# A two-layer decoder trunk on one core: the first two products in pair, the start of the loads rearranged, x's last quarter transposed by DMA

## The chip, the core and the metric

The kernel runs on one core of one Trainium2 chip. The metric is the time of one execution on the device, in microseconds (us); the number for a kernel is the median of several executions. Before the change it is 2162.82 us, the median of three runs.

## What is computed

Two layers over a sequence of 256 tokens with 2048 features. Each layer is a token mixer behind an RMS norm and then an MLP with squared ReLU behind an RMS norm, both added to the residual stream. The first layer's mixer, the part that this case is about, is attention with forget gates (FoX):

```python
D_MODEL = 2048; SEQ = 256; HEAD_DIM = 128; FOX_HEADS = 16

def fox_attention(h, w_in, b_f, q_gain, k_gain, w_out):   # h = rms_norm(x, mix_norm_g[0])
    proj = h @ w_in                                       # 2048 x (3*2048 + 16)
    q, k, v, f = jnp.split(proj, [H * dh, 2 * H * dh, 3 * H * dh], axis=-1)
    q = rms_norm(q.reshape(B, S, H, dh), q_gain)
    k = rms_norm(k.reshape(B, S, H, dh), k_gain)
    v = v.reshape(B, S, H, dh)
    log_f = jax.nn.log_sigmoid((f + b_f).astype(jnp.float32))
    c = jnp.cumsum(log_f, axis=1)
    ...
    s = jnp.einsum('bqhd,bkhd->bhqk', q_i, k) * scale
    s = s + jnp.transpose(c_i, (0, 2, 1))[..., None] - c_keys[:, :, None, :]
    p = jax.nn.softmax(jnp.where(causal, s, -jnp.inf), axis=-1)
    return jnp.einsum('bhqk,bkhd->bqhd', p, v)            # then @ w_out
...
def sq_relu_mlp(h, w_up, w_down):
    a = jax.nn.relu(h @ w_up)
    return (a * a) @ w_down
```

The second layer's mixer is a dilated sliding-window attention. All tensors are float32.

## The kernel before, in words

**Products.** Every large product is done in split precision: a weight tile `raw` (two blocks of 128 rows by 512 columns, 512 KB) is cast on ScalarE (ACT) to a rounded `wh` (`hi`, line 308), VectorE (DVE) subtracts it to get `wl` (`lo`, line 309), and TensorE does three matmuls per block of 128 rows and half of the tokens: activation-hi by weight-hi, activation-hi by weight-lo, activation-lo by weight-hi (lines 339 to 341). So one product of 256 tokens x 2048 rows x 512 columns (`product_steps`) is 16 row blocks x 2 halves of the tokens x 3 = 96 matmuls of 128x512. In this text the product matmuls are counted n = 0, 1, 2 and so on from the start. One product holds two of the four `ps_acc` banks of PSUM (`acc`).

**Order of the work.** `Jobs` is a small scheduler that runs while the program is built. Side work (normalization chains, attention heads) is written as Python generators that `yield` either a number of product steps to let pass or the name of a result to wait for. After each row block of a product `tick()` lets due jobs write their instructions. Each engine then does its instructions in that order, and an instruction that must wait holds up all behind it on the same engine. `behind(...)` and `issue_after` fix the order of two instructions.

**Loads.** `plan` lists the weight tiles in order of use; `load` issues one DMA of 512 KB, from SyncE's queue (SP), and `split` casts and subtracts one tile. `RAW_BUFS` and `W_BUFS` buffers bound how far they run ahead. At the start, `hold` keeps the loads after the first ones back: a DVE memset of one element of the target tile, ordered behind the copy of the norm gains (`gained`), stands before each of them.

**The start.** The first 256 KB loads of x and of the first weight tile go out on the queues of SP and ACT. The norm gains (`g_mix`, 16 KB) go out on GpSimd's (POOL) queue, and TensorE turns them into columns (`gain_columns`, line 137). Meanwhile `wake(8)` and later `wake(3)` do 128x128 transposes of an identity into a spare bank. x is in four column quarters `x0` to `x3`. For the first norm each quarter is transposed on TensorE (`ptx`, line 473, 32 transposes of 128x128 in all), and ACT (line 478) and DVE (line 479) multiply by the gain and split it into `hT` hi and lo. The later norms transpose x by DVE's 32x32 stream transposes and a pass of DMAs through DRAM (`transposed_by_dma`).

**The first layer's products.** For each of four groups j of four heads the q product, the k product and the v product follow one another; in group 0 the forget gates (`gate`, 32 matmuls of 128x256, line 639, tile `pf`) lie between q and k. After a product its chain runs beside the next ones: `qk_chain` squares the result on ACT (518), sums it on DVE (522), takes the power on POOL (`rq`, 525), normalizes (DVE 531, `qn`), does stream transposes (DVE 539, `sq`), writes four blocks of 64 KB to DRAM on SP (543), reads them back on POOL's queue (544, into `qn` again), and from there ACT makes `fqT`/`fkT` whole (`w`, 553) and hi (`h`, 560), DVE lo (`l`, 562), for each of two pairs of heads (`fkT_0`, `fkT_1`). The gate's chain makes `pft` (655), log-sigmoids on DVE (659 to 681, `g_z`, `g_u`, `g_s`), a cumulative sum by matmuls (`pc`, 684 to 686), its copy `c_q` (DVE 687), its transpose (`pct`, 691) and `negc` on DVE (693 to 702). `fox_head` starts with three kinds of matmul into `sc_f`: a selection matrix `sel` by `negc` (714), whole q by whole k (620), and the split parts (623). `make_sel(j)` builds `sel`: a POOL memset (747), two POOL selects (749) and a DVE cast (752); it is called at the head of each group's loop, ahead of its q product.

Of the kernel before, what the change touches and what calls it, by code (L numbers as in the profile page):

```python
# [38 lines left out]
CUT = 12  # L39

# [48 lines left out]
def trunk(ctx: ExitStack, tc, x, fox_w_in, fox_b_f, fox_q_gain, fox_k_gain, fox_w_out, dil_w_in,  # L89
# [17 lines left out]
    nc.scalar.activation(warm, warm, AF.Exp)  # L107
# [3 lines left out]
    nc.gpsimd.memset(mhalf, -0.5)  # L111


    spare = ps_sc.tile([P, P], F32, tag="sc", name="spare")

    def wake(times):
        for _ in range(times):
            nc.tensor.transpose(spare, ident, ident)

    wake(8)  # L120
# [20 lines left out]
    mix_rows = gain_rows("g_mix", [mix_norm_g.rearrange(per_chunk, p=P)], nc.gpsimd)  # L141

# [78 lines left out]
    def add_pair(*chunks):  # L221

        for rows in ((0, CUT * P), (CUT * P, D)):
            for w, cols in chunks:
                add(w, rows, cols)
# [6 lines left out]
    for j in range(4):  # L232
        for part in range(3):
            add(fox_w_in[0], (0, D), [(part * D + j * NC, NC)])
# [39 lines left out]
    raws, splits = [], []  # L274

    def load():
# [6 lines left out]
        for c, width in cols:  # L283
            src = w[r:r + RAW_SUB * P, c:c + width].rearrange("(c p) n -> p c n", p=P)
            if i:
                with hold(t[:, 0, 0:1]):
                    issued["load"] = nc.sync.dma_start(t[:, :, at:at + width], src)
            else:

                for part, queue in enumerate((nc.sync, nc.scalar)):  # L290
                    queue.dma_start(t[:, part, at:at + width], src[:, part, :])
            at += width
# [3 lines left out]
    def split():  # L296
# [9 lines left out]
        with behind(*([issued["gained"]] if i == 0 else issued.get("n0", []) if i < 2 * W_BUFS else [])):  # L306
            for part in ([slice(0, 1), slice(1, 2)] if i < 1 else [slice(0, W_SUB)]):
                issued["cast"] = nc.scalar.copy(hi[:, part, :], raw[:, part, :])  # L308
                issued["cut"] = nc.vector.tensor_sub(lo[:, part, :], raw[:, part, :], hi[:, part, :].bitcast(F32))  # L309
        splits.append((hi, lo))  # L310
        state["split"] += 1
# [17 lines left out]
    def product_steps(acc, keys, lhs, steps):  # L329

        for k in steps:
# [4 lines left out]
            for t in range(NT):  # L336
                tok = slice(t * P, (t + 1) * P)
                first, last = k == 0, k == KC - 1
                nc.tensor.matmul(acc[t], ah[:, tok], hi, start=first, stop=False)  # L339
                nc.tensor.matmul(acc[t], ah[:, tok], lo, start=False, stop=False)  # L340
                issued["product"] = nc.tensor.matmul(acc[t], al[:, tok], hi, start=False, stop=last)  # L341
            if i == W_SUB - 1:
                used[0] += 1
                split()
# [8 lines left out]
    def in_pair(new, steps, posts):  # L353
# [75 lines left out]
    def transposed_by_dma(tag, col, n):  # L429
# [3 lines left out]
        for t in range(NT):  # L433
            tile_ = work.tile([P, NC], F32, tag="w", name=f"turned_{tag}_{n}_{t}", bufs=5)
            blocks = dram.tile([4, 32, 4, P], F32, tag="blocks", name=f"blocks_{tag}_{n}_{t}", bufs=4)
            nc.vector.transpose(tile_.rearrange("p (j b r) -> p b j r", j=4, b=4),
                                xt[n][:, t, :].rearrange("p (b j c) -> p b j c", j=4, c=32))
# [3 lines left out]
            nc.sync.dma_start(tile_, blocks.rearrange("j c i x -> (j c) (i x)"))  # L441
            tiles.append(tile_)
        yield 9
# [17 lines left out]
    def norm_chain(tag, col, n, ssp, wait, later):  # L461
        yield wait
        if tag != "n0":
            yield from transposed_by_dma(tag, col, n)
        else:
            for half in range(2):
                pr = n * 2 + half
                pt = ps_tp.tile([P, 2, S], F32, tag="tp", name=f"ptx_{tag}_{pr}")
                with behind(*([issued["product"]] if "product" in issued else [])):
                    for i in range(2):  # L470
                        for t in range(NT):
                            c = (half * 2 + i) * P
                            issued["transposed"] = nc.tensor.transpose(
                                pt[:, i, t * P:(t + 1) * P], xt[n][:, t, c:c + P], ident)
                both = act.tile([P, 2, 2, S], F32R, tag="hT", name=f"hT_{tag}_{pr}", bufs=KC // 2)
                for i in range(2):
                    gc = gain[:, col + pr * 2 + i:col + pr * 2 + i + 1]
                    on_act = nc.scalar.activation(both[:, i, 0, :], pt[:, i, :], AF.Copy, scale=gc)
                    on_dve = nc.vector.scalar_tensor_tensor(both[:, i, 1, :], pt[:, i, :], gc,
                                                            both[:, i, 0, :].bitcast(F32), ALU.mult, ALU.subtract)  # L480
                issued[tag, pr] = issued[tag] = on_act, on_dve
# [428 lines left out]
    first = normed("n0", 0, lambda n: (0, 2, 6, 10)[n], lambda n: (13, 11, 9, 7)[n])  # L910

    def load_x(n):
        for t in range(NT) if n == 0 else [slice(0, NT)]:
            with hold(xt[n][:, 0, 0:1]):
                queue = nc.scalar if t == 1 else nc.sync
                issued["load"] = queue.dma_start(xt[n][:, t, :], xv[:, t, n * NC:(n + 1) * NC])

    def rest():
        while state["split"] - used[0] < W_BUFS:
            split()  # L920
            yield 1

    load_x(0)
    load()
# [7 lines left out]
    del issued["held"]  # L932
# [3 lines left out]
    split()  # L936
    for n in range(1, NX):
        jobs.spawn(first(n))
    jobs.spawn(rest())
    jobs.spawn(more_constants())  # L940
# [3 lines left out]
    for j in range(4):  # L944
        sel = make_sel(j)
# [56 lines left out]
```

## Time and profile before

| what | value |
| --- | --- |
| runs | 2163.41, 2161.27, 2162.82 us; median 2162.82 |
| profiled execution, its own time | 2161.91 us |
| its span on the core | 2160.2 us |
| granted TensorE clock, mean | 1.0 |
| TensorE busy | 2147.8 us, 99% |
| DVE busy | 1397.9 us, 65% |
| ACT busy | 1105.9 us, 51% |
| POOL busy | 74.1 us, 3% |
| data moved | 459.34 MB, mean 213 GB/s |

The profile is one execution. Its times count from the start of its span; the time on the device holds 1.7 us more than the span. A timeline row gives the start, the length, the engine, the line of the kernel, the operation and the tile it writes and reads; `x3` at the end says that three like instructions are drawn together. What stands in square brackets is the engine's idle time before the row and the instruction or DMA that ended it. `PE` is TensorE's matmul side, `PEld` its weight loads, `SPq`, `ACTq` and `POOLq` the sequencers that issue DMAs.

### The profile page before, as it was taken

What the parts mean: (1) busy time and instruction counts of PE and PEld (TensorE: products, weight loads), DVE (VectorE), ACT (ScalarE), POOL (GpSimd) and SP (SyncE); (2) the same over time, 40 slices, a digit from 0 to 9 for tenths busy, and PEclk for the clock granted to TensorE, in tenths of its full rate; (3) what the DMA queues carried; (4) which work ended last, traced back from release to release, by engine and by line L of the source; (5) the groups of instructions that cost most, each with busy time, mean ns of one, the idle gap of its engine ahead of it and who ended that gap; (6) DMA issues with size and microseconds to landing.
All of it is one profiled execution on the core that took longest, in us unless ns stands there. A gap on an engine that the chain in (4) does not pass through costs nothing.

```text
span 2160.2 us, 30057 instructions
## 1 busy us (share of the span) xinstructions
PE 2147.8 (99%) x11208; PEld 1912.6 (89%) x11208; DVE 1397.9 (65%) x1862; ACT 1105.9 (51%) x1545; POOL 74.1 (3%) x92
## 2 busy tenths in 40 slices
PE   9999999999999999999999999999999999999999
PEld 7888888988998998998888888888988988988988
DVE  6777787765655565566668777676655655655664
ACT  6565655644544454455555565546544543544442
POOL 1111000000000000000011010100000000000000
PEclk9999999999999999999999999999999999999999
DMA  7676667766666666667776776758666666666664
GB/s 251 220 225 196 224 201 233 248 203 204 199 203 205 200 201 204 203 199 241 244 242 207 232 226 195 259 177 275 215 204 201 200 204 204 198 203 204 202 210 144
DMA packets 292354, 459.34 MB, mean 213 GB/s; under 512 B 21944, under 2 KB 104432, under 8 KB 292208
## 3 DMA queue, kind: packets, MB, share of 16 engines
q1 hardware_dynamic: 288416, 446.27, 66.1%
q0 software_dynamic: 3232, 10.50, 1.4%
q8 instruction: 87, 1.43, 0.3%
q10 hardware_dynamic: 560, 0.66, 0.1%
q14 instruction: 59, 0.48, 0.1%
HBM read 438.48 MB, written 18.87 MB: 212 GB/s over the span
## 4 chain that ended last, share of the span: by engine, by line
PE 92%; DVE 3%; DMA 2%; issue 1%; ACT 1%; POOL 0%; SPq 0%; DVEq 0%; ACTq 0%; POOLq 0%
PE acc L340 19%; PE acc L341 19%; PE acc L339 19%; PE up_n1a_acc L403 5%; PE up_n3a_acc L403 5%; PE up_n3a_sc L403 3%; PE up_n1a_tp L403 3%; PE up_n1a_sc L403 3%; PE up_n3a_tp L403 3%; PE up_n3a_acc L407 3%; PE up_n1a_acc L407 3%; DMA raw<-in_dil_w_in_dram 2%; DVE wl L309 1%; PE up_n3a_tp L407 1%; PE up_n1a_sc L407 1%; PE up_n1a_tp L407 1%
## 5 line engine op out<-in xcount | busy, mean ns | idle before, releaser
L309 DVE TENSOR_TENSOR wl<-raw,wh 128x1024 fp32r<-128x1024 f32 (+1 forms) x801 | 975.0, 1221 | 686.7 <-ACT wh L308 681.0
L308 ACT CAST wh<-raw 128x1024 fp32r<-128x1024 f32 (+1 forms) x801 | 837.7, 1048 | 931.7 <-PE acc L341 567.4
L339 PE MATMUL acc<-wh,hT_n 128*128 128x512 f32 x896 | 343.0, 384 | 0.5 <-ACT wh L308 0.5
L340 PE MATMUL acc<-wl,hT_n 128*128 128x512 f32 x896 | 339.9, 379 | 0.1
L341 PE MATMUL acc<-wh,hT_n 128*128 128x512 f32 x896 | 339.5, 379 | 0.0
L339 PE MATMUL acc<-wh,aTh_n1a 128*128 128x512 f32 x512 | 194.0, 379 | 0.0
L340 PE MATMUL acc<-wl,aTh_n1a 128*128 128x512 f32 x512 | 194.0, 379 | 0.0
L341 PE MATMUL acc<-wh,aTl_n1a 128*128 128x512 f32 x512 | 194.0, 379 | 0.0
L341 PEld LDWEIGHTS acc<-wh,hT_n 128*128 128x128 f32 x896 | 169.3, 189 | 24.1
L339 PEld LDWEIGHTS acc<-wh,hT_n 128*128 128x128 f32 x896 | 169.6, 189 | 23.4 <-ACT wh L308 0.9
L340 PEld LDWEIGHTS acc<-wl,hT_n 128*128 128x128 f32 x896 | 169.8, 190 | 22.6 <-DVE wl L309 0.4
L339 PE MATMUL acc<-wh,aTh_n3a 128*128 128x512 f32 x480 | 181.9, 379 | 0.0
L340 PE MATMUL acc<-wl,aTh_n3a 128*128 128x512 f32 x480 | 181.9, 379 | 0.0
L341 PE MATMUL acc<-wh,aTl_n3a 128*128 128x512 f32 x480 | 181.9, 379 | 0.0
L403 PE MATMUL up_n1a_acc<-hT_n,wh 128*128 128x512 f32 x512 | 181.6, 382 | 0.0
L403 PE MATMUL up_n3a_acc<-hT_n,wh 128*128 128x512 f32 x512 | 181.6, 382 | 0.0
L407 PE MATMUL up_n1a_acc<-hT_n,wl 128*128 128x256 f32 x512 | 139.6, 273 | 0.0
L407 PE MATMUL up_n3a_acc<-hT_n,wl 128*128 128x256 f32 x512 | 139.6, 273 | 0.0
L341 PEld LDWEIGHTS acc<-wh,aTl_n1a 128*128 128x128 f32 x512 | 96.8, 189 | 13.8
L340 PEld LDWEIGHTS acc<-wl,aTh_n1a 128*128 128x128 f32 x512 | 96.8, 189 | 13.7
L339 PEld LDWEIGHTS acc<-wh,aTh_n1a 128*128 128x128 f32 x512 | 96.8, 189 | 13.6
L403 PEld LDWEIGHTS up_n3a_acc<-hT_n,wh 128*128 128x128 f32 x512 | 96.8, 189 | 13.5
(725 smaller groups left out, 3202.3 us busy)
## 6 DMA issues: line engine op xcount, KB each, us to landing
raw<-in_mlp_w_up_dram SPq DMA_DIRECT2D x256, 512.0 KB, 4.1
raw<-in_mlp_w_down_dram SPq DMA_DIRECT2D x256, 512.0 KB, 4.2
raw<-in_dil_w_in_dram SPq DMA_DIRECT2D x192, 256.0 KB, 4.6
raw<-in_fox_w_in_dram SPq DMA_DIRECT2D x95, 512.0 KB, 4.1
raw<-in_fox_w_out_dram SPq DMA_DIRECT2D x32, 512.0 KB, 4.3
raw<-in_dil_w_in_dram SPq DMA_DIRECT2D x32, 512.0 KB, 4.4
raw<-in_dil_w_out_dram SPq DMA_DIRECT2D x32, 512.0 KB, 4.4
blocks_n<-turned_n SPq DMA_DIRECT2D x96, 64.0 KB, 2.4
```

The source lines that it names most:

```text
L308: issued["cast"] = nc.scalar.copy(hi[:, part, :], raw[:, part, :])
L309: issued["cut"] = nc.vector.tensor_sub(lo[:, part, :], raw[:, part, :], hi[:, part, :].bitcast(F32))
L339: nc.tensor.matmul(acc[t], ah[:, tok], hi, start=first, stop=False)
L340: nc.tensor.matmul(acc[t], ah[:, tok], lo, start=False, stop=False)
L341: issued["product"] = nc.tensor.matmul(acc[t], al[:, tok], hi, start=False, stop=last)
L403: issued["product"] = nc.tensor.matmul(banks[b], hi[:, i, col], in_turn(tokens.rearrange("p x s -> p (x s)"), P // 2), start=first, stop=last)
L407: nc.tensor.matmul(banks[b][:, 0:S], lo[:, i, col], in_turn(tokens[:, 0, :], P // 2), start=False, stop=False)
```

## The change

- The q and k products of group 0 are done in pair: q's row blocks 0 to 11, k's row blocks 0 to 11, then q's 12 to 15 and k's 12 to 15. The gate stands between the two second parts. All four `ps_acc` banks are held until the pair ends. The plan of the loads follows this order. `make_sel(0)` is called behind the pair.
- x's last quarter (row blocks 12 to 15 of the products) is transposed by `transposed_by_dma` in the first norm too, with its last reads on POOL's queue; eight transposes of TensorE go.
- First loads: x's quarter 0 in two halves of columns on SP; the first weight tile's halves on ACT's queue and SP's; the norm gains on ACT's queue. The next loads are paced by memsets of whole target tiles on POOL, each behind the one before, in place of the memsets behind the gains; two more loads follow behind the last of these.
- The first weight tile is cast and subtracted in two halves, the second behind the first pair's `hT`.
- The transposes of a pair of row blocks go to two PSUM banks, one of each pool, in place of one.
- The wake matmuls are 128x512 products of zeros (six, then three), not 128x128 transposes (eight, then three).

```diff
+FIRST_CUT = 12
...
-    spare = ps_sc.tile([P, P], F32, tag="sc", name="spare")
+    spare = ps_sc.tile([P, NC], F32, tag="sc", name="spare")
+    zeros = work.tile([P, NC], F32R, tag="w", name="zeros", bufs=5)
+    nc.vector.memset(zeros.bitcast(F32), 0.0)
...
-            nc.tensor.transpose(spare, ident, ident)
-    wake(8)
+            nc.tensor.matmul(spare, zeros[:, 0:P], zeros, start=True, stop=True)
+    wake(6)
...
-    mix_rows = gain_rows("g_mix", [mix_norm_g.rearrange(per_chunk, p=P)], nc.gpsimd)
...
+        chunks = [(fox_w_in[0], [(part * D + j * NC, NC)]) for part in range(3)]
+        if j == 0:
+            add_pair(*chunks[0:2], cut=FIRST_CUT)
+        for w, cols in chunks[2 if j == 0 else 0:]:
+            add(w, (0, D), cols)
...
-    def hold(first):
+    def hold(whole):
         if "held" not in issued:
             return ExitStack()
-        with behind(issued["gained"]):
-            nc.vector.memset(first, 0.0)
-        return behind(*([issued["load"]] if issued["held"] == [] else []))
+        with behind(*issued["held"]):
+            issued["held"] = [nc.gpsimd.memset(whole, 0.0)]
+        return behind(issued["load"])
...
-    def in_pair(new, steps, posts):
+    def in_pair(new, steps, posts, cut=CUT, between=lambda: None):
         banks = []
         for n in range(2):
             banks.append(new(n))
-            steps(banks[n], range(CUT))
+            steps(banks[n], range(cut))
         for n in range(2):
-            steps(banks[n], range(CUT, KC))
+            steps(banks[n], range(cut, KC))
             jobs.spawn(posts[n](banks[n]))
+            if n == 0:
+                between()
...
-    def transposed_by_dma(tag, col, n):
+    def transposed_by_dma(tag, col, n, queue, steps, *order):
...
-            nc.sync.dma_start(tile_, blocks.rearrange("j c i x -> (j c) (i x)"))
+            queue.dma_start(tile_, blocks.rearrange("j c i x -> (j c) (i x)"))
...
-            yield from transposed_by_dma(tag, col, n)
+            yield from transposed_by_dma(tag, col, n, nc.sync, 9)
+        elif n == NX - 1:
+            yield from transposed_by_dma(tag, col, n, nc.gpsimd, 15, cuts[6], issued["n0"][1])
...
-                pt = ps_tp.tile([P, 2, S], F32, tag="tp", name=f"ptx_{tag}_{pr}")
+                pt = [pool.tile([P, S], F32, tag=x, name=f"ptx_{tag}_{pr}_{x}") for pool, x in ((ps_tp, "tp"), (ps_sc, "sc"))]
...
-    first = normed("n0", 0, lambda n: (0, 2, 6, 10)[n], lambda n: (13, 11, 9, 7)[n])
+    first = normed("n0", 0, lambda n: (0, 2, 5, 7)[n], lambda n: (12, 12, 11, 1)[n])
...
+    nc.sync.dma_start(*halves_x[0])
+    with behind(nc.scalar.dma_start(first_raw[:, 0, :], first_w[:, 0, :])):
+        mix_rows = gain_rows("g_mix", [mix_norm_g.rearrange(per_chunk, p=P)], nc.scalar)
+        nc.scalar.activation(warm, warm, AF.Exp)
+    with behind(nc.sync.dma_start(first_raw[:, 1, :], first_w[:, 1, :])):
+        issued["load"] = nc.sync.dma_start(*halves_x[1])
...
-    issued["held"] = True
-    for what in (load, lambda: load_x(1), load, lambda: load_x(2), load, lambda: load_x(3), load):
+    with behind(issued["load"]):
+        load()
+    issued["held"] = [ready]
+    for what in (lambda: load_x(1), load, load, lambda: load_x(2), load):
         what()
-        issued["held"] = []
     del issued["held"]
+    split_row_block(0)
     jobs.spawn(first(0))
     with behind(issued["transposed"]):
         wake(3)
-    split()
+    with behind(*issued["n0"]):
+        split_row_block(1)
...
+    for what in (load, lambda: load_x(3)):
+        with behind(issued["load"]):
+            what()
...
-        sel = make_sel(j)
+        sel = make_sel(j) if j else None
...
+        if j == 0:
+            in_pair(lambda n: sums(), lambda acc, ks: product_steps(acc, keys_h(tag), lhs_h(tag), ks),
+                    [q_post, k_post], FIRST_CUT, gates)
+            sel = make_sel(j)
+        else:
+            product(keys_h(tag), lhs_h(tag), q_post)
+            product(keys_h(tag), lhs_h(tag), k_post)
```

More of the change, by code (lines that the diff above doesn't have):

```diff
@@ L106, in trunk @@
     nc.gpsimd.memset(warm, 0.0)
-    nc.scalar.activation(warm, warm, AF.Exp)
     ident = const.tile([P, P], F32, name="ident")
@@ L284, in load @@
             src = w[r:r + RAW_SUB * P, c:c + width].rearrange("(c p) n -> p c n", p=P)
[L285 to L291, printed above, removed]
+            with hold(t):
+                issued["load"] = nc.sync.dma_start(t[:, :, at:at + width], src)
             at += width
@@ L305, in split @@
         lo = wpool.tile([P, W_SUB, NC], F32R, tag="wl", name=f"wl{i}", bufs=W_BUFS)
[L306 to L309, printed above, removed]
+        with behind(*(issued.get("n0", []) if i < 2 * W_BUFS else [])):
+            issued["cast"] = nc.scalar.copy(hi, raw)
+            issued["cut"] = nc.vector.tensor_sub(lo, raw, hi.bitcast(F32))
         splits.append((hi, lo))
+        cuts.append(issued["cut"])
         state["split"] += 1
@@ L338, in product_steps @@
                 first, last = k == 0, k == KC - 1
-                nc.tensor.matmul(acc[t], ah[:, tok], hi, start=first, stop=False)
+                with behind(*([issued["product"]] if first and 0 < used[0] < W_BUFS else [])):
+                    nc.tensor.matmul(acc[t], ah[:, tok], hi, start=first, stop=False)
                 nc.tensor.matmul(acc[t], ah[:, tok], lo, start=False, stop=False)
```

72 lines of the change are left out of this document (44 added, 28 removed).

## The prediction

> **What bounds the kernel now.** I read the page first, then TensorE's waits, then the timeline at the two places that the change touches.
>
> ```profile
> span 2160.2 us, 30057 instructions
> ## 1 busy us (share of the span) xinstructions
> PE 2147.8 (99%) x11208; PEld 1912.6 (89%) x11208; DVE 1397.9 (65%) x1862; ACT 1105.9 (51%) x1545; POOL 74.1 (3%) x92
> ```
>
> ```profile
> PE ps_g_mix L137 <- DMA g_mix<-in_mix_norm_g_dram: 2.1, 1, 2.1
> ```
>
> TensorE is busy for 2147.8 of 2160.2 us. So time can only come from TensorE instructions that go away or from the few places where TensorE waits, and time is lost where a new wait is made. In the list of its waits the longest that the change touches is the one above, for the norm gains at the start; a second, for the first FoX head, is shown with its rows further down. The whole stake is a few microseconds in 2162, and 0.2% is 4.3 us, about what a measurement of this kernel can tell from no change: faster is under 2158.5, slower over 2167.15.
>
> The start, from the timeline (start, length, engine, line, tile; idle time before it and what ended that), engine by engine: TensorE, GpSimd, ACT, DVE.
>
> ```profile
> 6.62 0.31 PE L137 MATMUL ps_g_mix<-ident,g_mix 32*128 32x32 f32 x1 [2.11 <-DMA g_mix<-in_mix_norm_g_dram]
> 6.86 1.11 PE L473 MATMUL ptx_n<-ident,x 128*128 128x128 f32 x4
> 7.76 0.85 PE L118 MATMUL spare<-ident 128*128 128x128 f32 x3
> 8.53 0.80 PE L339 MATMUL acc<-wh,hT_n 128*128 128x512 f32 x1
> 9.12 0.63 PE L340 MATMUL acc<-wl,hT_n 128*128 128x512 f32 x1
> 9.55 0.59 PE L339 MATMUL acc<-wh,hT_n 128*128 128x512 f32 x1
> 9.97 0.38 PE L340 MATMUL acc<-wl,hT_n 128*128 128x512 f32 x1
> 10.19 0.59 PE L341 MATMUL acc<-wh,hT_n 128*128 128x512 f32 x2
> ...
> 19.91 0.46 PE L339 MATMUL acc<-wh,hT_n 128*128 128x512 f32 x1
> ```
>
> ```profile
> 1.42 0.66 POOL L130 DMA_DIRECT2D g_mix<-in_mix_norm_g_dram  x1 [0.33 <-issue]
> ...
> 3.03 1.34 POOL L749 TENSOR_SCALAR_AFFINE_SELECT self<-self 128x512 f32<-128x512 f32 x2
> ```
>
> ```profile
> 8.01 0.47 ACT L478 ACTIVATE hT_n<-ptx_n,gain 128x256 fp32r<-128x256 f32 x1 [0.68 <-PE ptx_n L473]
> ...
> 11.91 1.04 ACT L308 CAST wh<-raw 128x1024 fp32r<-128x1024 f32 x1 [0.17 <-DMA raw<-in_fox_w_in_dram]
> ```
>
> ```profile
> 4.41 0.44 DVE L752 CAST sel<-self 128x512 fp32r<-128x512 f32 x1 [4.41 <-POOL self L749]
> ...
> 45.03 1.22 DVE L309 TENSOR_TENSOR wl<-raw,wh 128x1024 fp32r<-128x1024 f32 x1
> ```
>
> The gain row's DMA, issued on POOL at 1.42, releases TensorE at 6.62. The first product is at 8.53. Starts 9.55 and 9.97 lie 0.42 us apart, 9.97 and 10.19 only 0.22 (to more digits 0.2157, the pitch I use): the clock came up at 9.97, after TensorE had been at work steadily since 6.62. The row at 19.91 is product matmul n = 36, counting the 128x512 product matmuls from 0.
>
> **Part 1, the start.** The gain rows now go out on ACT's hardware queue, behind a 256 KB half of the first weights. I bound their landing by these rows:
>
> ```profile
> x<-in_x_dram ACTq DMA_DIRECT2D x1, 256.0 KB, 4.0
> ...
> g_mix<-in_mix_norm_g_dram POOLq DMA_DIRECT2D x1, 16.0 KB, 5.2
> ```
>
> From above: no sooner than before, 6.6. From below: an ACT-queue DMA issued at 0.81 has landed after 4.0, at 4.8. The ACT-queue row is the nearest, so I take 5.0. Then come the gain transpose (0.24, from 6.62 to 6.86), the first x transposes (0.90, to 7.76) and three 128x512 wake matmuls at the cold 0.42 (1.28, they were 128x128): first product at 7.4, 1.1 earlier. The Trainium skill, "DMA: Bandwidth & Descriptors", section "Latency and other measured facts", gives 600 ns to the first byte for a hardware queue and about 1 us for GpSimd's. By that figure the gain rows would come only 0.4 us earlier, at 6.2, the first product would be at 8.6, and 1.2 us of this part's gain would be gone; the 4.0 against the 5.2, with the issue 0.6 earlier, says more than that, and I keep the rows.
>
> From 7.4 to n = 36: 36 products x 0.2157 = 7.8; 20 transposes in that stretch (16 before) at 0.109, half of a 256-column pitch, = 2.2; cold pitch up to the same 9.97, half of 2.6 = 1.3 (0 if the six wide wake matmuls bring the clock up before, which the narrow eight did not); and a wait for the second weight chunk. That one is now split behind the first pair's hT: 0.47 + 0.47 + 1.04 + 1.22 = 3.2 us of ACT and DVE against some 2.2 us of TensorE work, so 1.0 (0 to 2). Sum 19.7, against 19.91: -0.2. And of x's 32 transposes eight are gone and four that came later are done by then: 12 x 0.109 = 1.3 less afterwards. **Early gain 1.5 us**, between -1.1 (gain rows no sooner than 6.6, the second chunk's wait at 2) and 4.0 (gain rows at 4.8, the clock up, no such wait).
>
> What the quarter's new path needs costs nothing as long as it lies beside TensorE's matmuls: two stream transposes, eight block DMAs on SP, two DMAs on POOL, 8 ACT and 8 DVE operations of 128x128 for x's last quarter. That quarter holds rows 12 to 15, which the pair uses only after row 11 of k, and by the order of the queues I estimate 3.6 us in hand; if that cover is gone, the third rival has its price. Likewise the third and fourth ps_acc banks: v's first product now waits until q's result is read out, with some 0.6 us to spare by my estimate; if it waits, that time is part of the DVE time counted next and not added to it.
>
> **Part 2, head 0.** The first head's scores need the k product normalized, and that chain runs mainly on DVE:
>
> ```profile
> 65.15 0.36 DVE L529 TENSOR_SCALAR rq_('fk', 0)_723<-rq_('fk', 0)_723,rstd_n 128x4 f32<-128x4 f32 x2 [1.78 <-POOL rq_('fk', 0)_723 L525]
> ...
> 72.75 0.38 DVE L562 TENSOR_TENSOR fqT_1l<-sq_('fq', 0)_0_525,fqT_1h 128x256 fp32r<-128x256 f32 x1
> ```
>
> ```profile
> 73.19 0.53 POOL L747 MEMSET self<- 128x512 f32 x1 [8.08 <-DVE fqT_1l L562]
> 73.80 2.54 POOL L749 TENSOR_SCALAR_AFFINE_SELECT self<-self 128x512 f32<-128x512 f32 x2
> 76.29 0.60 POOL L544 DMA_DIRECT2D qn_('fk', 0)_0_771<-blocks_('fk', 0)_0_777  x1
> ```
>
> ```profile
> 81.91 0.51 ACT L553 ACTIVATE fkT_0w<-qn_('fk', 0)_0_771,gain 128x256 f32<-128x256 f32 x1 [1.87 <-DMA qn_('fk', 0)_0_771<-blocks_('fk', 0)_0_777]
> ```
>
> ```profile
> 85.26 0.33 PE L714 MATMUL sc_f<-negc,sel 128*128 128x384 f32 x1
> 85.43 0.38 PE L620 MATMUL sc_f<-fkT_0w,fqT_0w 128*128 128x128 f32 x2
> 86.96 0.38 PE L623 MATMUL sc_f<-fkT_0h,fqT_0h 128*128 128x256 f32 x1 [1.15 <-ACT fkT_0h L560]
> ```
>
> From the split at 45.03 to the end of fqT_1l at 73.13 DVE has 28.1 us of queued work: q's chain, k's chain, the gate's small operations and nine weight splits. Then POOL builds the next selection table (memset and two selects), and only behind it issues k's block read; the read takes 5.6 and ACT begins fkT_0w at 81.91. So fqT_1l to fkT_0w is 8.8 us. TensorE reaches the head at 85.26 and waits there 1.15 us in the row at 86.96, with smaller gaps before and behind it 1.7 us in all.
>
> Before, TensorE had 96 k products and the gate between q's end and k's end. In the pair q ends at n = 167 and k at n = 191, only 24 products later, and the two chains fall on DVE together. Let E be q's end. DVE's list until fqT_1l is the same 28.1, and: +1.3, because the wait for POOL's rq of k (1.78 in the row) and that of q are no longer both covered by splits that are there to be done; +0.41 and +0.44, the copy of the gate's result and the cast of the first selection table (4.41 row), which now lies behind the pair; -0.6, part of q's square sums that come before E. It starts 1.25 after E, when ACT has squared q's first half and the split in hand is done. So fqT_1l ends at E + 30.9, fkT_0w starts 8.8 later at E + 39.7, and TensorE can do its head product at E + 40.1 (half a microsecond of ACT). TensorE without a wait gets there after 147 products x 0.2157 = 31.7, nine gate matmuls at half that, 1.0, and the gate's and head's small matmuls, 1.8: E + 34.5. **It waits 5.6 us** (3.0 to 7.0), of which about 1.0 falls at the gate's transpose pct, whose operand c_q is copied on DVE behind rq of k and a split, and 4.6 in one stretch at the head. The old 1.7 goes: **+3.9**. What is late next is the weighted sum of head 0 and head 1's transposes, since two heads' DVE work is then bunched: +0.2, between 0 and 0.8.
>
> The waiting instruction stands in TensorE's one queue, so everything behind it, the v products too, waits; DVE and ACT do splits meanwhile, and come out of the wait with more chunks in stock, so nothing else is lost. Paced loads move SP's later loads earlier than the gain did; they were not the bound after n = 36 and I cost them at nothing.
>
> **Sum.** The profiled run took 2161.91 (span 2160.2 and 1.7 around it). -1.5 + 3.9 + 0.2 = +2.6, so 2164.5. The median of before, 2162.82, is 0.9 above that run: forecast 2165.4, inside 0.2%.
>
> **The rivals.**
>
> *The idle stretch costs the clock too (slower).* After the start TensorE's longest stretch without work in this trace is the 1.15 us at 86.96, and no row shows what a longer one does. At the start the clock was down until TensorE had worked 3.35 us (6.62 to 9.97); a second such stretch at half clock costs 1.7, and up to double if the gate comes late, so +2.5: 2167.9, over the bound. It decides from the idle length at which the gate closes, against my 4.6. The Trainium skill, "TensorE: Matmul & The Clock Gate", section "What's actually happening", says that the clock halves after about 3.4 us of idle, counted in a free-running window. By that rule a 4.6 us stretch closes the gate only in those phases in which a whole window fits into it, and a wait of under 3.4 never does; the trace's 1.15 us without a change agrees and cannot decide. Chance 0.24.
>
> *The k chain is in time (faster).* If the selects take 1.34 as at 3.03 instead of 2.54, the block read takes about 3.8 instead of 5.6, as this row of the second group of heads has it, and two of the nine splits fall behind the chain (1.2 each), 5.4 us go and the head does not wait.
>
> ```profile
> qn_('fq', 1)_0_1276<-blocks_('fq', 1)_0_1282 POOLq DMA_DIRECT2D x1, 256.0 KB, 3.8
> ```
>
> ```profile
> GB/s 0 52 297 328 175 0 41 233 239 367 377 411 383 400 392 392 392 382 382 283 61 17 85 252 367 398 400 398 385 252 210 328 293 18 234 197 221 192 234 177
> ```
>
> Then -1.5 - 1.7: 2159.6; with the clock up early at the start (1.3 more) 2158.3. Against it: all three must happen, and in this trace the rows beside the chain show none of them. Chance 0.22, half of it under the bound.
>
> *Loads come late.* The GB/s row (1.25 us a slice, first 50 us) shows the DMA engines at about 400 for most of 11 to 24 us. x's last quarter now goes out to blocks and back in, 1.05 MB more, 2.6 us at that rate, in just this stretch, and the weight load for rows 10 and 11 stands on SP's queue behind the loads of the gate's weights and bias. By the order of the queues I estimate 1 to 2 us in hand; if that is too much by as much, TensorE waits 1 to 3 us before n = 144: about 2167.4. Chance 0.10.
>
> The change might also do nothing of what it says: the first products may start no earlier if the gain rows land at 6.2 or later. That takes 1.2 off the gain, 2166.6, and lies inside the forecast's own range.
>
> **How the numbers follow.** Forecast 0.44, its own range 2163 to 2168 (the early gain down to its half or up to 2.5 and the wait between 4 and 7, not all at the worst end at once), with 0.10 of it over 2167.15. Clock rival 0.24, of it 0.19 over. Loads 0.10, 0.07 over. In time 0.22, 0.12 under 2158.5. Slower 0.10 + 0.19 + 0.07 = 0.36, faster 0.12, the rest 0.52. The range leaves out 0.12 below 2158.5 and some 0.08 above 2169.5, the clock rival with both its bounds.
>
> **What would show it.** Right: the gain's transpose on TensorE near 5.0 and the first product near 7.4; eight fewer ptx transposes; a wait of 4 to 5 us before the first head's fkT_0w product, released by ACT, and one of about 1 before pct; n = 36 near 19.7. Wrong: no wait at the head; product starts 0.42 apart behind the wait; a wait of a product for wh released by a raw DMA between 20 and 45 us; or a gain transpose no earlier than 6.2.

## The result, and the profile after

The changed kernel takes 2167.88 us (median of 8 runs, 2165.64 to 2169.53), the kernel before 2161.82 (8 runs, 2160.04 to 2163.67). The ratio is 1.0028, 95% interval 1.0017 to 1.0039: 6.1 us slower, or 0.28%. The forecast was 2165.4 with a range of 2158.5 to 2169.5; the time is that of its clock rival, and over the 0.2% that the prediction called slower (chance 0.36). The profiled run took 2167.86, its span is 2166.0.

The page of the changed kernel, and below it the list of TensorE's waits (in total, how often, longest):

```profile
span 2166.0 us, 30067 instructions
...
PE 2151.1 (99%) x11198; PEld 1914.9 (88%) x11198; DVE 1400.6 (65%) x1862; ACT 1105.4 (51%) x1549; POOL 79.8 (4%) x98
```

```profile
PE sc_f L631 <- ACT fkT_0w L564: 4.6, 1, 4.6
PE ps_g_mix L139 <- DMA g_mix<-in_mix_norm_g_dram: 2.1, 1, 2.1
...
PE pct L702 <- DVE c_q L698: 1.0, 1, 1.0
```

Two entries of 1 us or more are new in kind: 4.6 at the first head's product of whole q and k, and 1.0 at the gate's transpose (the 1.5 left out is the first wake matmul's, 2.5 before). TensorE's busy time went up by 3.3 us with ten matmuls fewer. By the windows view 1.5 of that lies before product n = 192, where the wake matmuls are wider, and 2.7 between n = 300 and 360. The timeline around the first head, in that stretch, shows slow matmuls:

```profile
88.45 0.38 PE L340 MATMUL acc<-wl,hT_n 128*128 128x512 f32 x1
93.46 0.79 PE L631 MATMUL sc_f<-fkT_0w,fqT_0w 128*128 128x128 f32 x2 [4.63 <-ACT fkT_0w L564]
93.90 0.77 PE L341 MATMUL acc<-wh,hT_n 128*128 128x512 f32 x1
94.47 0.63 PE L339 MATMUL acc<-wh,hT_n 128*128 128x512 f32 x1
94.90 0.63 PE L340 MATMUL acc<-wl,hT_n 128*128 128x512 f32 x1
...
97.88 0.50 PE L341 MATMUL acc<-wh,hT_n 128*128 128x512 f32 x1
98.22 0.38 PE L339 MATMUL acc<-wh,hT_n 128*128 128x512 f32 x1
```

From 94.47 to 97.88 products start 0.43 apart, twice 0.2157. The windows view puts the granted clock beside it (the column after POOL's busy time; then the DMA engines' busy share and GB/s):

```profile
88.00:90.00 2.00, 0.83 (x4) 0.38 (x2) 1.11 (x1) 0.00 (x0) 0.90 (x2) 1.00 1.02 391
90.00:92.00 2.00, 0.00 (x0) 0.00 (x0) 0.00 (x0) 0.00 (x0) 0.00 (x0) 0.83 1.02 333
92.00:94.00 2.00, 0.54 (x3) 0.55 (x3) 0.00 (x0) 1.10 (x3) 0.00 (x0) 0.50 1.01 396
94.00:96.00 2.00, 2.00 (x7) 1.64 (x6) 1.34 (x3) 1.39 (x3) 0.00 (x0) 0.50 0.23 86
96.00:98.00 2.00, 2.00 (x6) 1.55 (x6) 0.65 (x1) 0.00 (x0) 0.00 (x0) 0.50 0.13 11
98.00:100.00 2.00, 2.00 (x12) 1.81 (x11) 0.50 (x1) 1.58 (x3) 0.00 (x0) 0.97 0.72 251
```

0.83 in the second row means that the clock fell to half at about 91.3; by the 0.97 in the last it came back at about 98.1. What releases the head is the chain that the prediction followed, on POOL (table, then the block reads) and ACT:

```profile
84.73 0.53 POOL L758 MEMSET self<- 128x512 f32 x1 [6.63 <-DVE fqT_1l L573]
85.33 2.48 POOL L760 TENSOR_SCALAR_AFFINE_SELECT self<-self 128x512 f32<-128x512 f32 x2
87.77 0.59 POOL L555 DMA_DIRECT2D qn_('fk', 0)_0_770<-blocks_('fk', 0)_0_776  x1
```

```profile
92.90 0.51 ACT L564 ACTIVATE fkT_0w<-qn_('fk', 0)_0_770,gain 128x256 f32<-128x256 f32 x1 [6.17 <-DMA qn_('fk', 0)_0_770<-blocks_('fk', 0)_0_776]
```

At the start, TensorE and the DMA issues on ACT:

```profile
6.59 0.28 PE L139 MATMUL ps_g_mix<-ident,g_mix 32*128 32x32 f32 x1 [2.14 <-DMA g_mix<-in_mix_norm_g_dram]
...
8.99 0.63 PE L339 MATMUL acc<-wh,hT_n 128*128 128x512 f32 x1
...
12.26 0.72 PE L339 MATMUL acc<-wh,hT_n 128*128 128x512 f32 x1
12.82 0.38 PE L340 MATMUL acc<-wl,hT_n 128*128 128x512 f32 x1
13.03 0.38 PE L341 MATMUL acc<-wh,hT_n 128*128 128x512 f32 x1
```

```profile
0.81 0.45 ACTq L938 DMA_DIRECT2D raw<-in_fox_w_in_dram  x1
1.29 0.48 ACTq L132 DMA_DIRECT2D g_mix<-in_mix_norm_g_dram  x1
```

The gains release TensorE at 6.59, where it was 6.62 before, and the fast pitch begins only at 12.82.

Where the 5.8 us between the two spans lie, by the start of the same product matmul n (lines 339 to 341) in both traces (after less before): at n = 192, when both have done the same products, +0.3; at n = 300, behind pct, +1.5; at n = 360, from where the order of TensorE's instructions is the same, +7.6; at the end +5.9. The last 1.7 come back in the second layer's attention (n = 3860 to 4670), where the profile of before has a second wait at sc_d (0.6) and a short one at ptp_d (0.1) which the profile after does not have. The change has no part in that: no profile of an experiment has the 0.6 either, not even that of `before_gain` (below), which has the instructions of before there and stands at -0.06 against it at n = 2600 and at -1.6 at n = 4670. Whether the kernel before often waits so, or only in this execution, is open. From 300 to 360 the gaps over the usual pitch come to some 5.9 of these 6.1: 4.8 of wait (the row's 4.63 and the restart), 0.3 behind it, 2.2 of slow pitch in ten products, 0.4 at the split scores, less the 1.8 of before.

### The profile page after: what moved, and what is told of

Read it like the earlier page. It is cut to its first block, busy times and chain, and to the rows that moved or that the text cites. A ratio compares the mean times of both kernels' runs of the same rounds, so it can differ in the third digit from the quotient of the medians.

```text
span 2166.0 us, 30067 instructions
## 1 busy us (share of the span) xinstructions
PE 2151.1 (99%) x11198; PEld 1914.9 (88%) x11198; DVE 1400.6 (65%) x1862; ACT 1105.4 (51%) x1549; POOL 79.8 (4%) x98
## 4 chain that ended last, share of the span: by engine, by line
PE 96%; DVE 2%; DMA 1%; issue 1%; ACT 0%; POOL 0%; SPq 0%; ACTq 0%; POOLq 0%; DVEq 0%
PE acc L340 20%; PE acc L341 20%; PE acc L339 20%; PE up_n1a_acc L406 5%; PE up_n3a_acc L406 5%; PE up_n1a_sc L406 3%; PE up_n1a_tp L406 3%; PE up_n3a_sc L406 3%; PE up_n3a_tp L406 3%; PE up_n3a_acc L410 3%; PE up_n1a_acc L410 3%; PE up_n3a_tp L410 1%; PE up_n3a_sc L410 1%; PE up_n1a_tp L410 1%; PE up_n1a_sc L410 1%; DVE wl L307 1%
## 5 line engine op out<-in xcount | busy, mean ns | idle before, releaser
L307 DVE TENSOR_TENSOR wl<-raw,wh 128x1024 fp32r<-128x1024 f32 x799 | 973.9, 1223 | 684.0 <-ACT wh L306 681.1
L306 ACT CAST wh<-raw 128x1024 fp32r<-128x1024 f32 x799 | 835.6, 1048 | 933.0 <-PE acc L341 569.2
```

The costliest lines, as they stand in the source:

```text
L306: issued["cast"] = nc.scalar.copy(hi, raw)
L307: issued["cut"] = nc.vector.tensor_sub(lo, raw, hi.bitcast(F32))
```

## The experiments

Each is a kernel of its own, compared with the kernel before on the same chip; the changed kernel itself is at 2167.88. The kernel before had medians of 2161.4 to 2161.7 in these comparisons. Differences between two changed kernels are by their medians, a rough measure: the interval of each against before is 2 to 3 us to either side.

**Selection tables behind k's reads** (`sel_late`). The POOL memset of the next table is ordered behind the last block read:

```diff
-            nc.gpsimd.dma_start(qn[t], blocks...)
+            issued["read"] = nc.gpsimd.dma_start(qn[t], blocks...)
...
-        nc.gpsimd.memset(sf, 0.0)
+        with behind(*([issued["read"]] if j else [])):
+            nc.gpsimd.memset(sf, 0.0)
```

> The changed kernel, with POOL's build of the next selection table (memset and two selects) forced behind the two block reads of k. TensorE's order is that of the changed kernel. Theory A (the head's wait is set by the chain DVE fqT_1l, POOL's table, POOL's block read, ACT; and its 4.63 us of idleness closes the clock): the read is issued about 3.1 us earlier, the wait before the first head's fkT_0w product falls from 4.63 to about 1.5, no product behind it starts 0.43 apart, and the time falls by 3.1 + 2.3 = 5.4, from 2167.9 to about 2162.5. Theory B (the read is limited by the DMA engines, not by its issue): the read lands where it did, nothing gained, 2167 to 2168. Theory C (the clock loss has nothing to do with the length of the idle stretch): 3.1 gained, slow pitch stays, 2164.8.

2162.88 us, ratio to before 1.0006 (0.9997 to 1.0015): 5.0 won, and no longer to be told from before. POOL, and TensorE's timeline at the head:

```profile
84.13 0.59 POOL L555 DMA_DIRECT2D qn_('fk', 0)_0_770<-blocks_('fk', 0)_0_776  x1 [7.41 <-DMA blocks_('fk', 0)_0_776<-sq_('fk', 0)_0_723]
```

```profile
89.28 0.49 PE L631 MATMUL sc_f<-fkT_0w,fqT_0w 128*128 128x128 f32 x2 [1.83 <-ACT fkT_0w L564]
89.52 0.46 PE L341 MATMUL acc<-wh,hT_n 128*128 128x512 f32 x1
89.82 0.38 PE L339 MATMUL acc<-wh,hT_n 128*128 128x512 f32 x1
```

The read now waits for its blocks and not for POOL, the head waits 1.83, and the products behind it keep the pitch of 0.2157. Theory A holds: the table cost about 3 us in the chain, and the rest of the 5.0 is the clock. That the clock stayed up behind the head is seen in this one execution. Five of the 11 runs have a mean granted clock of 0.999, which is what one stretch of 3.4 us at half clock makes of 2160 us; in the profiled one, one of the five, that stretch lies at the start, from 7.8 to 11.2.

**Work in the wait** (`fill`). The first head's first matmul is done 20 times more.

```diff
-        yield (3 if j == 3 else 4) * hh + 2
+        yield (3 if j == 3 else 4) * hh + (2 if h else 3)
...
+            for _ in range(0 if h else 20): nc.tensor.matmul(ps[:, 0:3 * P], sel[:, hh, :], in_turn(negc, P // 2), start=True, stop=True)
```

> The changed kernel, with the first head's first matmul (128x384) done 20 times more, each overwriting the last, one row block later, so that TensorE works for 3.3 of the some 5 us in which it would wait; the end of the wait stays where ACT's fkT_0w sets it. Theory A (idleness closes the clock): an idle stretch of about 2 us is left, products behind it start 0.216 apart, and the time falls by 1.3 to 2.3 (the split scores now stand nearer behind the wait and may wait up to 1.0), to about 2166. Rival (the clock falls for another reason, such as the kind of work or the DMA load): slow pitch stays, no change, 2168 or more.

2170.38 us, 1.0038 (1.0026 to 1.0051): by the medians 2.5 worse than the changed kernel, not better (the two intervals overlap). The edit moved the head's split scores up behind the whole product, where they wait for ACT too:

```profile
92.86 0.49 PE L631 MATMUL sc_f<-fkT_0w,fqT_0w 128*128 128x128 f32 x2 [1.88 <-ACT fkT_0w L564]
93.10 0.46 PE L339 MATMUL acc<-wh,hT_n 128*128 128x512 f32 x1
93.40 0.38 PE L340 MATMUL acc<-wl,hT_n 128*128 128x512 f32 x1
93.61 0.38 PE L341 MATMUL acc<-wh,hT_n 128*128 128x512 f32 x1
96.15 0.58 PE L634 MATMUL sc_f<-fkT_0h,fqT_0h 128*128 128x256 f32 x1 [2.16 <-ACT fkT_0h L571]
96.52 0.63 PE L339 MATMUL acc<-wh,hT_n 128*128 128x512 f32 x1
```

As a test of "one long stretch" it failed, but its timeline says more than the time does: behind the first wait of 1.88 the pitch is fast (93.40, 93.61), behind the second of 2.16 it is slow (96.52 on), though neither is half as long as 4.63. So one unbroken wait is not needed. Nor is a loaded DMA, which the rival named: the clock falls in this row of the windows (0.94), and the DMA engines are idle in it (busy share 0.01).

```profile
94.00:96.00 2.00, 0.00 (x0) 0.00 (x0) 1.48 (x3) 2.00 (x5) 0.00 (x0) 0.94 0.01 3
```

That it goes by how little is done in a stretch of some 3.4 us fits these rows; it is a reading of them, with its figures in the next section, and not a test.

**Heads later** (`heads_later`). The first group's heads begin four row blocks later:

```diff
-        yield (3 if j == 3 else 4) * hh + 2
+        yield (3 if j == 3 else 4) * hh + (6 if j == 0 else 2)
```

> The changed kernel, with the four heads of the first group begun four row blocks (24 products, 5.2 us) later. Theory A: the wait of 4.63 at the first head goes or is under 1, the clock stays up, and 4.6 + 2.3 are won: about 2161, if the heads' ends find room in the next q product. Rival (the bunched DVE work of four heads and of the next group makes new waits behind): waits at the transposes or products of the later heads of 2 to 4 us, 2163 to 2165.

2169.79 us, 1.0035 (1.0021 to 1.0048). Nothing was won; the time is over the rival's 2163 to 2165 too. Its waits:

```profile
PE sc_f L634 <- ACT fkT_0h L571: 3.1, 1, 3.1
...
PE ptp_f L605 <- DVE s_f L744: 1.6, 1, 1.6
...
PE sc_f L631 <- ACT fkT_0w L564: 1.4, 1, 1.4
```

The scheduler that orders TensorE's queue now put the split scores close behind the whole product, so the wait of 4.6 became 1.4 and 3.1, with three products between. The clock fell all the same (half from 96.3 to 103.2 in its windows), and a wait at a later head's transposes, the 1.6, came on top. That is more than the rival foresaw, which had waits at the later heads alone.

**Gains first** (`gain_first`). The gains' DMA goes ahead of the first weight half on ACT's queue:

```diff
-    with behind(nc.scalar.dma_start(first_raw[:, 0, :], first_w[:, 0, :])):
-        mix_rows = gain_rows("g_mix", [...], nc.scalar)
-        nc.scalar.activation(warm, warm, AF.Exp)
+    mix_rows = gain_rows("g_mix", [...], nc.scalar)
+    with behind(issued["rows"]): first_half = nc.scalar.dma_start(first_raw[:, 0, :], first_w[:, 0, :])
+    with behind(first_half): nc.scalar.activation(warm, warm, AF.Exp)
```

> The changed kernel, with the norm gains' DMA ahead of the first weight half on ACT's queue, not behind it. In the changed kernel the gains release TensorE at 6.59, no earlier than before. Theory A (the 16 KB stood in the queue behind 256 KB): the gain transpose starts between 3.5 and 5.0, the first product 1.5 to 2.5 earlier than at 8.99 unless the first weight half, 0.5 later, holds it, and the time falls by 1 to 2, to about 2166.4. Theory B (16 DMA engines busy with 1 KB pieces delay every queue alike): the gain transpose still starts after 6.0 and the time stays at 2167.5 to 2168.5.

2166.44 us, 1.0023 (1.0014 to 1.0033), 1.4 under the changed kernel by the medians; this was not resolved between the two directly. The DMA view (KB each, median us to landing) and ACT's timeline:

```profile
g_mix<-in_mix_norm_g_dram ACTq DMA_DIRECT2D x1, 16.0 KB, 2.6
```

```profile
6.55 0.62 ACT L958 CAST wh<-raw 128x512 fp32r<-128x512 f32 x1 [3.26 <-DMA raw<-in_fox_w_in_dram]
```

The gains land 2.6 after their issue at 0.81, so at 3.4, and the gain transpose is at 4.38, right behind the wake matmuls. So it is the place behind the 256 KB, with an issue 0.48 later, that held them in the changed kernel. Whether the queue's order did it or the load that all DMA engines have by then is not separated: in the kernel before the gains were alone in POOL's queue, issued at 1.42, and released TensorE at 6.62 too. The first product then waits 1.5 for what the weight half holds up, and starts at 7.59.

**The start alone** (`start_only`): no pair (q, gate, k as before, plan and tables too), x's last quarter on TensorE and the order of the first norm as before, everything else of the change kept.

```diff
-        if j == 0:
-            add_pair(*chunks[0:2], cut=FIRST_CUT)
-        for w, cols in chunks[2 if j == 0 else 0:]:
+        for w, cols in chunks:
...
-        elif n == NX - 1:
-            yield from transposed_by_dma(tag, col, n, nc.gpsimd, 15, cuts[6], issued["n0"][1])
...
-            in_pair(lambda n: sums(), ..., [q_post, k_post], FIRST_CUT, gates)
-            sel = make_sel(j)
+            product(keys_h(tag), lhs_h(tag), q_post)
+            gates()
+            product(keys_h(tag), lhs_h(tag), k_post)
```

> The changed kernel without the pair and with x's last quarter transposed by TensorE again: of the change only the new first loads, the gains on ACT's queue, the wide wake matmuls and the two banks for transposes are left. Theory A (the start is worth little either way, as the gains land no earlier and the first product comes at 7.7 to 9.0 by the clock's phase; the loss is the pair's): 2161 to 2163 against 2161.7 of before, the first head's wait as before, under 2. Rival (the start itself loses, by the 1 KB pieces of x's two column halves and the later clock): 2163 to 2165.

2160.67 us, 0.9997 (0.9988 to 1.0006): no difference that this measurement resolves, and by the median just under both ranges. The first head waits 1.0. The start did not lose the 6 us.

**The pair alone** (`pair_alone`): the kernel before with q and k in pair, plan, gate and first table as in the change.

```diff
+            in_pair(lambda n: sums(), lambda acc, ks: product_steps(acc, keys_h(tag), lhs_h(tag), ks),
+                    [q_post, k_post], gates)
+            sel = make_sel(j)
```

> The kernel before, with the first q and k products in pair behind row 12 and the first selection table behind the pair; start and transposes as before. Theory A (the pair brings q's and k's chains onto DVE together): the wait of some 4.6 at the first head's fkT_0w product and one of 1 at pct appear, the clock falls behind it in most runs: 2161.7 + 6 to 8, 2168 to 2170. Rival (the loss needs the new start or the DMA path of x's last quarter, whose SP and POOL transfers delay k's blocks): wait under 3, 2162 to 2165.

2166.88 us, 1.0025 (1.0016 to 1.0035). Its waits and one row of its windows:

```profile
PE sc_f L625 <- ACT fkT_0w L558: 4.9, 1, 4.9
```

```profile
92.00:96.00 4.00, 3.32 (x9) 2.77 (x10) 1.99 (x3) 2.49 (x5) 0.00 (x0) 0.50 0.31 119
```

The pair alone makes the wait and the clock loss, and 5.4 of the 6 us; that is about 1 under theory A's 2168 to 2170. The wait at pct is not in its list: that part of theory A was wrong.

**The quarter on TensorE** (`pe_quarter`): the changed kernel without the two lines that send x's last quarter through `transposed_by_dma`.

> The changed kernel with x's last quarter transposed by TensorE, the pair and all else kept. Theory A (the DMA path puts some 1.4 us of stream transposes and eight short subtractions onto DVE, ahead of the norm's square sums, and so makes the 1.2 us wait at pct): the wait at pct goes, TensorE has 8 transposes of 0.109 more, the first head's wait of 4.6 stays with the clock loss behind it: 2167.9 - 1.2 + 0.9 less the chain's head start of 0 to 1, 2166.5 to 2167.6. Rival (the pct wait is the pair's own, since c_q stands behind k's chain): pct wait stays at 1.0 to 1.2, 2168.5 to 2169.

2166.74 us, 1.0023 (1.0014 to 1.0032). The list of TensorE's waits has 4.5 at sc_f and no pct. So the DMA path, which takes eight transposes off TensorE (0.9), is what makes pct wait (1.0). By the medians it costs 1.1, which the intervals do not resolve. The likely way, argued and not tested alone, is DVE's queue: two stream transposes and, in this row of the changed kernel's groups from 40 to 60 us, eight subtractions:

```profile
L459 DVE SCALAR_TENSOR_TENSOR hT_n<-turned_n,gain,hT_n 128x128 fp32r<-128x128 f32 x8 | 2.2, 347 | 0.0
```

What pct waits for, `c_q`, stands on DVE behind k's `rq` and a split in the changed kernel (the first two rows); in `pe_quarter` (the last row) DVE waits for TensorE there.

```profile
74.55 0.36 DVE L540 TENSOR_SCALAR rq_('fk', 0)_731<-rq_('fk', 0)_731,rstd_n 128x4 f32<-128x4 f32 x2 [1.78 <-POOL rq_('fk', 0)_731 L536]
...
75.95 0.18 DVE L698 COPY c_q<-pc 128x32 f32<-128x32 f32 x1
```

```profile
73.75 0.19 DVE L696 COPY c_q<-pc 128x32 f32<-128x32 f32 x1 [0.73 <-PE pc L695]
```

**The changed kernel mended** (`pair_best`): `sel_late`, `gain_first` and pct two row blocks later (`yield 3` for `yield 1` behind `c_q`).

> The changed kernel with the two edits that gained, the selection tables behind k's block reads and the gains first on ACT's queue, and the gate's transpose pct two row blocks later. Theory A (the three are independent): 2167.9 - 5.0 - 1.4 - 1.2 = 2160.3; no wait at pct, the first head's wait under 1.5, the clock stays up. Rival (each only moves the same wait: head 0 then waits for DVE, whose list is as long as before): 2161.5 to 2163.

2161.94 us, 1.0005 (0.9996 to 1.0013). The rival held: the wait moved. With pct later, `negc` is later on DVE, and the head's first matmul waits for that:

```profile
88.11 0.57 PE L725 MATMUL sc_f<-negc,sel 128*128 128x384 f32 x1 [2.69 <-DVE negc L713]
88.48 0.63 PE L340 MATMUL acc<-wl,hT_n 128*128 128x512 f32 x1
```

```profile
88.00:90.00 2.00, 1.89 (x5) 1.64 (x6) 1.67 (x1) 0.42 (x1) 0.59 (x1) 0.55 1.00 394
```

And 2.69 us were enough for the slow clock in this execution: the granted clock is 0.55 in the two us behind the wait.

**The kernel before with the same two edits** (`before_two`), and each alone (`before_gain`, `before_sel`). The gains go first on ACT's queue, ahead of its halves of x and of the first weights; ACT's table load moves behind these; the tables as in `sel_late`.

```diff
-    mix_rows = gain_rows("g_mix", [mix_norm_g.rearrange(per_chunk, p=P)], nc.gpsimd)
+    mix_rows = gain_rows("g_mix", [mix_norm_g.rearrange(per_chunk, p=P)], nc.scalar)
...
     load()
+    with behind(issued["first"]): nc.scalar.activation(warm, warm, AF.Exp)
```

> The kernel before with two edits of the same kind: the gains first on ACT's queue (ACT's table load behind its three loads), the selection tables behind k's block reads. Theory A: the gain transpose starts at 4.4 to 5.0 and the first product 1.0 to 1.5 earlier; the first head's 1.7 goes; 2161.7 - 1.2 - 1.7 = 2158.8, under before and under the changed kernel. Rival (x's first half, now second on ACT's queue, holds the transposes, and the first head then waits for DVE): 2160.5 to 2161.7.

> The kernel before with the gains first on ACT's queue alone (the table load behind ACT's three loads). Theory A (the two edits of before_two are independent): gain transpose at about 4.3, first product about 7.5, 2161.5 - 1.3 = 2160.2. Rival (the earlier start is eaten by weight loads that come no earlier): 2161.0 to 2161.7.

> The kernel before with the selection tables behind k's block reads alone. Theory A: the first head's waits of 1.7 go, nothing new: 2161.5 - 1.7 = 2159.8. Rival (the reads land no earlier, or later groups lose what the first wins): 2161.0 to 2162.

`before_two` 2158.36 us, 0.9987 (0.9978 to 0.9996); `before_sel` 2159.25, 0.9990 (0.9981 to 0.9999); `before_gain` 2160.36, 0.9992 (0.9983 to 1.0001), not resolved. By the medians -2.2 and -1.1 alone and -3.1 together: they add up within the noise. What the gains first are worth alone is open: in `before_gain`'s profile the first product starts 0.6 earlier, but n = 36 at the same time as before: TensorE waits 1.8 for x's half, and the fast pitch begins at 11.5, not at 10.0. In `before_two` n = 36 is 1.2 earlier, no wait at the first head is left in the list, and the start reads (TensorE):

```profile
4.29 0.31 PE L136 MATMUL ps_g_mix<-ident,g_mix 32*128 32x32 f32 x1 [0.39 <-DMA g_mix<-in_mix_norm_g_dram]
4.54 0.48 PE L472 MATMUL ptx_n<-ident,x 128*128 128x128 f32 x1
5.87 0.90 PE L472 MATMUL ptx_n<-ident,x 128*128 128x128 f32 x3 [0.85 <-DMA x<-in_x_dram]
```

Here x's half, now second on ACT's queue, takes back 0.85 of what the gains won.

**The change's start with both edits** (`start_two`): `start_only` with `sel_late` and `gain_first`.

> The start of the change without pair and without the DMA path, with both gaining edits: gains first on ACT's queue, selection tables behind k's block reads. Theory A (all add up): 2160.7 - 1.4 - 1.7 = 2157.6, as good as or better than before_two's 2158.4. Rival (the first weight half, second on ACT's queue, holds the first product, as it did in gain_first by 1.5): 2158.5 to 2159.5.

2158.63 us, 0.9984 (0.9975 to 0.9993): the rival's range, no better than `before_two`, with a wait of 1.4 before the first product. Both are under the kernel before and under the changed one.

## Why the prediction was right or wrong

- **The head's wait** was right in mechanism and size: 1.0 at pct and 4.6 at the head were forecast, 1.0 and 4.63 measured. The steps of the chain hold too: q's last product ends at 53.6 (the prediction's E), fqT_1l 31.0 later (forecast 30.9), and the head's product starts 39.9 later (forecast 40.1). `pair_alone` shows that the pair makes the second wait, and `sel_late` that POOL's table lies in its chain. One reason was wrong: at pct, c_q does stand behind k's rq and a split on DVE, as forecast (74.55, 75.95), but that comes with x's quarter on DVE. Without it k's rq is done by 69 and pct does not wait (`pe_quarter`). So the 1.0 that came out right there is luck.
- **The clock** was the rival at 0.24, and it came. Its condition, 4.6 us of idleness being too much, held; its price of 2.5 was close to the 2.2 measured. What failed is the step from a wait to its price in the forecast: the idle stretch alone was charged. All 8 runs of the changed kernel have a mean granted clock of 0.997 to 0.999 where 17 of 20 runs of before have 1.000 (one stretch of 3.4 us at half clock makes 0.999, the two of the changed kernel's profile 0.998). So the likeliest case should have had it. The Trainium skill, "TensorE: Matmul & The Clock Gate", section "What's actually happening", speaks of an idle window of about 3.4 us; by that rule waits of under 3.4 cost no clock. Here 2.69 did in one execution and two waits of 1.88 and 2.16 with five matmuls between them in another, while 1.83 alone, in `sel_late`, did not, so the measurement speaks for a window in which little was done. An estimate from the windows view, over the 3.4 us before each fall at the head: 0 to 1.1 us of work in seven profiles, with 1.6 in the stretch of `sel_late` that kept its clock (steps of 3.41 from its fall at 7.8). The limit is not fixed by that: at the start the clock fell in four profiles behind stretches with 1.3 to 1.9 us of work (`sel_late`, `pe_quarter`, `pair_best`, `start_two`).
- **The early gain** failed: -1.5 forecast; +0.3 at n = 192 in the profile after. Two terms were mis-sized. The gains were put at 5.0 by the row of an ACT-queue DMA that was first in its queue, and came at 6.59: that they stand behind 256 KB was said but not priced (`gain_first`: landed at 3.4, transpose at 4.38). And the clock was to come at 9.97 as before; it came at 12.8 here. The four profiles with this same start code (`after`, `sel_late`, `fill`, `heads_later`) have n = 192 at +0.3, -1.2, -0.4 and -0.4 against before, with the lasting fast pitch beginning between 10.5 and 12.8. So the start, with its fewer transposes, gains some 0.4 on average, and single profiles differ by 1.5. The rule of the Trainium skill on first bytes ("DMA: Bandwidth & Descriptors", "Latency and other measured facts"), by which the gains come at 6.2 by the prediction's estimate, was nearer than my row here; but with the gains first in the same hardware queue they landed at 3.4, which 0.4 us would not give.
- **The transposes**: ten matmuls fewer in all (eight transposes, two wake matmuls), as read from the diff. That their cover costs nothing was wrong: with the DMA path came the wait at pct (`pe_quarter`), about as long as what was saved; that it comes by the 16 short operations and two stream transposes is argued.
- **What comes behind the head** (+0.2) was 0.4, and **late loads** did not happen: no product waits for a weight load between 20 and 45 us.

The range held, but the size did not: +2.6 was forecast, and 6.1 came. Two of the prediction's own signs of being wrong were seen: products 0.43 apart behind the wait, and a gain transpose later than 6.2. From profile to profile the miss is some 3.3 us: 2.2 of clock left out, 1.8 from the early gain (-1.5 forecast, +0.3 measured) and 1.0 in smaller terms, less the 1.7 that came back in the second layer. The forecast's time is off by 2.5 only, because it started from a median of three runs, 0.9 above the profiled run, that 8 runs put 1.0 lower. That the measured time equals the clock rival's to 0.1 is therefore partly chance: the rival had the clock right, but its early gain and its baseline were off.

## What to carry to other kernels

A wait of a few microseconds on the busiest engine has to be priced with the clock that it may close: here 4.6 us of waiting cost 7, and splitting the wait or filling it in part did not help. Doing two products in pair puts their side chains onto the other engines together, and the first user of both results then waits for the two; beginning that user 24 products later did not cure it here (`heads_later`). A small transfer that all wait for goes out first, and a table that nobody needs yet goes behind the transfers on the queue of its engine: together these two edits took 3.1 us off the kernel before by the medians (0.9 to 4.8 by the interval), where the whole change lost 6.

## What the runs showed of the hardware that was not expected

A wait of 2.69 (`pair_best`), and a pair of waits of 1.88 and 2.16 close together (`fill`), were each followed by half the clock for 3.4 us in the windows view, and one of 4.63 by half the clock from 91.3 to 98.1, two such stretches, of which TensorE worked 4.6 us. Every slow stretch behind the start in these profiles has one of these two lengths, 3.4 or 6.8. Behind the waits of over 4 us the clock came back only after a second stretch, though TensorE had worked 1.3 to 2.5 us in the first. At the start a clock that was already up fell again behind waits of 1.4 to 2.3 us in four profiles, in `sel_late` from 7.8 to 11.2. And 16 KB issued 0.48 us behind 256 KB in one hardware queue released its user at 6.59; issued ahead of it, it had landed by 3.4.
